# Turns of v, the keys and i by VectorE's 32 by 32 blocks and a trip through DRAM, in a hybrid RWKV-7 / HGRN2 decoder step

## The chip, the cores and the metric

The kernel runs on one core of one Trainium2 chip. The metric is the device time in microseconds (us), median of three runs: 1077.69 us before the change (1077.2 to 1079.74). A core has five engines with their own in-order instruction streams: TensorE (PE in the profile; its weight loads are PEld), VectorE (DVE), ScalarE (ACT), GpSimd (POOL) and SyncE (SP), which here only issues DMAs.

## The reference

One layer, 256 prompt tokens and 8 sequences of 8 new tokens, together NT = 320 columns; D = 2048. Cut to what matters:

```python
h = rms_norm(x, norm_g)
p = einsum('nld,dp->nlp', h, w_in)               # 2048 x 12416: most of the work
r, k, v = token-shifted columns of p             # 16 heads of 64
S_t = S_{t-1} diag(w_t) - (S_{t-1} kk_t)(kk_t a_t)^T + v_t k_t^T ;  y_t = S_t r_t     # branch A
S_t = diag(g_t) S_{t-1} + k_t i_t^T ;  o_t = S_t^T q_t                                # branch B
merged = sigmoid(gate_a) * (y_a @ proj_a) + sigmoid(gate_b) * (y_b @ proj_b)
y = x + merged @ w_out ;  final RMSNorm
```

Both recurrences are computed in chunks, as products of small matrices. All numbers are float32; a large product is three passes over a split into a high and a low part.

## The kernel before, in words

**Stages.** A start stage normalises and turns x. Then comes the recorded stage, `record_all` (lines 1533 to 1590), which fills most of the first 661 us: for each of eight pairs of heads it computes eight tiles of 128 columns of the input projection (`tile_of`, 48 matmuls into the tile `mps` each) and runs `rwkv` for two heads of branch A and `hgrn` for one of branch B. Seven further tiles, the first seven of gate a, follow the eighth pair and give TensorE something to do while the last pair ends. The last stages compute the other gates, the two branch projections (`ppa`, `ppb`) and the output projection (`po`).

**The order.** In the recorded stage nothing is issued directly. The class `Recorder` collects all operations with what they read and write (`link`), gives each an assumed cost, and lists them by a simulated greedy order (`order`); that list is then emitted, so each engine's stream is fixed when the program is built. TensorE's big matmuls keep their own order, and the products of the recurrences are set between them where their data is assumed to be ready. For a DMA that touches a DRAM scratch (names with `scr`) the recorder assumes 4.5 us until a reader may start, and 6.5 us for the large one (line 170). DMAs of this stage all stand in SP's stream, the weight loads `raw` among them.

**Turns on TensorE.** Some operands are needed with tokens in the partitions and come with tokens in the columns. `rwkv` turns v by three transposes into `pv` and two ScalarE copies into `uv` (lines 967 to 973), and the keys `bk2` and `bks` by five transposes into `pbt` and `pbs` and two copies into `bk` (1107 to 1114). `hgrn` turns i (called `v` there) by three transposes into `pvt` and two copies into `vt` (1324 to 1330). In the profile they are `bank<-ident,v`, `bank<-ident,bk`, `bank<-ident,bks` and `bank<-ident,i`.

**The inverse through DRAM.** `rwkv` inverts small triangular matrices on VectorE. The products `g2` (from `bank<-arp,bk`) are copied to `nd` (tile `big`), written to DRAM (`scr<-big`, `scrs<-dns`), read back in another layout into `U`, which is the tile `wide_` (`ww<-scr`, `ww<-scrs`), worked on by a chain of small VectorE operations, written and read again (`scr<-xc`, `ye<-scr`, `uQ<-scr`), turned in 32 by 32 blocks on VectorE (`uK<-ye`) and used in the products `bank<-yz,uE` and those behind it, the chain over chunks.

**Homes.** Tiles are buffers by tag. The tile `wide_` serves, one after the other, `uS` (columns 0 to 383), `uB` (384 to 767), `pp` with `rv` (from 768), and `U`. The tag `big` serves `nd`, `t3`, `bm` and, at the end of a pair, `sg`. Four early gates stay in `sga`; three go to DRAM (`late`, in the profile `scrg`) from buffers of `za`, `q` and `f` of the pair before the last, and come back as `ga` at line 1635. A helper emits all recorded operations, so that they have line 198 in the profile.

Of the kernel before, what the change touches and what calls it, by code (L numbers as in the profile page):

```python
# [17 lines left out]
NP_ = 256  # L18
# [22 lines left out]
NFILL = 4  # L41
NLATE = 3
# [28 lines left out]
def blocks_of(ap):  # L71

    seen = {ap.offset}
    for st, cnt in [tuple(x) for x in ap.ap]:
        if st:
            seen = {c + st * j for c in seen for j in range(cnt)}
    return ap.tensor.name, 0, 1, sum(1 << b for b in {c // 1024 for c in seen})


class Recorder:  # L80
# [17 lines left out]
    def add(self, eng, name, fn, args, kw):  # L98
# [49 lines left out]
        elif eng == "V":  # L148
# [6 lines left out]
            if name == "tensor_tensor_scan":  # L155
                o.cost = 2 * free / 0.96 + 157
        elif eng == "S":
# [269 lines left out]
def hybrid_step(ctx, tc, x_prompt, x_sample, state_rwkv, state_hgrn, state_shift, norm_g, w_in,  # L427
# [68 lines left out]
    def run(gen):  # L496
        for _ in gen:
            pass
# [323 lines left out]
    sga = ypool.tile([128, max(NFILL, 1), NT], F32, name="sga", tag="sga")  # L822
# [9 lines left out]
    def ring(pool, tag, shape, bufs, dt, size, clear=False):  # L832
# [17 lines left out]
        if len(shape) == 2:  # L850
# [4 lines left out]
    SIZES = {"uK": 384, "uS": 384, "uE": 384, "uA": 320, "uB": 384, "uQ": 320, "pp": 256, "fd": NT, "big": 512, "s0t": 512, "v": 384,  # L855
             "w1": 384, "w2": 320, "w3": 320, "ks": 128, "ket": 256, "o": NT}
# [55 lines left out]
    def rwkv(p, r, k, vp, za):  # L912
        c = lambda base: cols[:, base + p:base + p + 1]
        v = vp[:, 64:]
# [12 lines left out]
        V.tensor_scalar(kk, k, c(KK_), 0.0, op0=ALU.mult, op1=ALU.add)  # L927
# [53 lines left out]
        bk2 = at("bk2", (128, 5, 2, 64))  # L981
        blocks = bk2[:, 0:4].rearrange("p (a c) j t -> p a (c j) t", c=2)
        b64 = lambda t_: t_[:, :NP_].rearrange("p (a c t) -> p a c t", a=2, c=2)
        V.tensor_mul(blocks[:, :, 0:4:3], b64(e2), b64(be))
        V.tensor_mul(bk2[:, 4, 0], e2[:, NP_:], be[:, NP_:])
# [11 lines left out]
        V.tensor_mul(bk2[:, 4, 1], e2[:, NP_:], a[:, NP_:])  # L997
# [9 lines left out]
        bks = at("bks", (128, 2, 2, 32))  # L1007
        for a_ in range(2):
            V.tensor_mul(bks[:, a_].rearrange("p j (s i) -> p j s i", i=8),
                         bk2[:, 4, :, 32 * a_:32 * a_ + 32].rearrange("p j (s i) -> p j s i", i=8),  # L1010
                         f[:, None, 8 + 4 * a_:12 + 4 * a_, None].to_broadcast([128, 2, 4, 8]))


        az = at("az", (128, 2, 2, 96))
        rz = at("rz", (128, 4, 2, 2, 8))
        for h in range(2):
            for s_ in range(2):
# [12 lines left out]
                        bk2[HS[h], ci].rearrange("p j t -> p (j t)"), arp[HS[h], ci, :, h]),  # L1030
# [11 lines left out]
        quads = [slice(32 * q_, 32 * q_ + 32) for q_ in range(4)]  # L1042
# [120 lines left out]
        def chunks():  # L1163
            st_ = None
            for ci in range(4):
# [123 lines left out]
        sg = at("sg", tag="big")  # L1289
# [20 lines left out]
    def hgrn(hd, q, k, v, zb):  # L1310
# [186 lines left out]
    prompt_ = [scr.tile([512, 32], F32, name=f"scr{j}", tag=f"scr{j}") for j in range(2)]  # L1497
# [322 lines left out]
```

## Time and profile before

| what | value |
|---|---|
| median of three runs | 1077.69 us (1077.2 to 1079.74) |
| the profiled execution's own time | 1079.4 us |
| its span, first to last instruction | 1077.5 us |
| TensorE busy, weight loads busy | 98%, 95% of the span |
| VectorE, ScalarE, GpSimd busy | 71%, 65%, 11% |
| recorded stage | from about 27 us to about 661 us of the span |

The profile names the writing and read tiles of each instruction as out<-in. Busy matmuls overlap: a matmul's duration (about 310 ns for 320 columns) is longer than the distance to the next one, so distances of starts, not durations, add up to time.

### The profile page before, as it was taken

To read this page: it belongs to the slowest core of one execution; us is meant where nothing else is said; L and a number is where in the kernel's file an instruction comes from. 1 tells how busy PE (TensorE), PEld (TensorE's weight loads), DVE (VectorE), ACT (ScalarE), POOL (GpSimd) and SP (SyncE) were. 2 spreads that over 40 slices of the span, in tenths; PEclk is the share of its full clock that TensorE was granted. 3 is DMA by queue.
4 is the path that set the end of the run, shared out by engine and by line. 5 is a ranking of instruction groups with operands and counts; after the bars stand their busy time and mean duration, and the time that the engine had idled before them with its cause. 6 is when DMAs were issued, how large, how long until landed. Compare 5 with 4: busy or idle time off the path is not lost.

```text
span 1077.5 us, 23000 instructions
## 1 busy us (share of the span) xinstructions
PE 1057.9 (98%) x8828; PEld 1022.9 (95%) x8828; DVE 759.8 (71%) x1640; ACT 703.2 (65%) x1608; POOL 122.6 (11%) x366
## 2 busy tenths in 40 slices
PE   7999999999999999999999999999999999999996
PEld 6999999999998999999999999999999999988886
DVE  8888989988897889889898956545444444446632
ACT  7758878877967868969879778444444444434412
POOL 9410301201202112012012000000000000000000
PEclk9999999999999999999999999999999999999998
DMA  6764564563653754654735646545545555587502
GB/s 201 191 164 127 160 164 129 146 177 110 183 163 90 185 160 120 168 146 119 200 107 162 184 115 190 156 144 157 156 141 154 154 143 154 154 276 240 189 20 98
DMA packets 302353, 166.98 MB, mean 155 GB/s; under 512 B 39261, under 2 KB 291424, under 8 KB 301668
## 3 DMA queue, kind: packets, MB, share of 16 engines
q1 hardware_dynamic: 301876, 164.21, 53.7%
q8 instruction: 69, 1.13, 0.4%
q10 hardware_dynamic: 368, 1.31, 0.3%
q14 instruction: 40, 0.33, 0.1%
HBM read 154.07 MB, written 11.42 MB: 154 GB/s over the span
## 4 chain that ended last, share of the span: by engine, by line
PE 96%; DVE 1%; ACT 1%; issue 1%; DMA 1%; POOL 0%; DVEq 0%; ACTq 0%
PE mps L198 47%; PE bank L198 11%; PE mps L493 5%; PE mps L492 5%; PE mps L491 5%; PE po L1693 3%; PE po L1691 3%; PE po L1692 3%; PE ppb L492 2%; PE ppb L493 2%; PE ppb L491 2%; PE ppa L493 2%; PE ppa L492 2%; PE ppa L491 2%; PE po L1697 1%; PE po L1696 1%
## 5 line engine op out<-in xcount | busy, mean ns | idle before, releaser
L198 PE MATMUL mps<-hlo,whi 128*128 128x320 f32 x1136 | 357.5, 315 | 0.0
L198 PE MATMUL mps<-hhi,whi 128*128 128x320 f32 x1136 | 356.3, 314 | 0.0
L198 PE MATMUL mps<-hhi,wlo 128*128 128x320 f32 x1136 | 356.0, 313 | 0.0
L198 PEld LDWEIGHTS mps<-hlo,whi 128*128 128x128 f32 x1136 | 214.0, 188 | 1.7 <-issue 1.2
L198 PEld LDWEIGHTS mps<-hhi,whi 128*128 128x128 f32 x1136 | 213.9, 188 | 1.6 <-issue 0.8
L198 PEld LDWEIGHTS mps<-hhi,wlo 128*128 128x128 f32 x1136 | 214.0, 188 | 0.9 <-issue 0.4
L198 DVE TENSOR_TENSOR wlo<-raw,whi 128x1024 fp32r<-128x1024 f32 x140 | 172.0, 1228 | 20.6 <-ACT whi L198 18.3
L481 ACT CAST whi<-raw 128x1024 fp32r<-128x1024 f32 x82 | 86.1, 1051 | 146.6 <-PE mps L492 93.4
L198 ACT CAST whi<-raw 128x1024 fp32r<-128x1024 f32 x140 | 146.2, 1044 | 50.6 <-PE mps L198 45.3
L482 DVE TENSOR_TENSOR wlo<-raw,whi 128x1024 fp32r<-128x1024 f32 x82 | 100.4, 1225 | 111.1 <-ACT whi L481 111.0
L491 PE MATMUL mps<-hhi,whi 128*128 128x320 f32 x400 | 123.6, 309 | 0.0
L492 PE MATMUL mps<-hlo,whi 128*128 128x320 f32 x400 | 123.6, 309 | 0.0
L493 PE MATMUL mps<-hhi,wlo 128*128 128x320 f32 x400 | 123.6, 309 | 0.0
L491 PEld LDWEIGHTS mps<-hhi,whi 128*128 128x128 f32 x400 | 75.1, 188 | 0.0
L492 PEld LDWEIGHTS mps<-hlo,whi 128*128 128x128 f32 x400 | 75.1, 188 | 0.0
L493 PEld LDWEIGHTS mps<-hhi,wlo 128*128 128x128 f32 x400 | 75.1, 188 | 0.0
L1679 ACT CAST whi<-raw 128x1024 fp32r<-128x1024 f32 x32 | 33.2, 1051 | 47.7 <-DMA raw<-in_w_out_dram 26.0
L1680 DVE TENSOR_TENSOR wlo<-raw,whi 128x1024 fp32r<-128x1024 f32 x32 | 38.5, 1223 | 36.0 <-ACT whi L1679 30.7
L1693 PE MATMUL po<-wlo,mhi 128*128 128x512 f32 x128 | 50.1, 391 | 0.0
L1691 PE MATMUL po<-whi,mhi 128*128 128x512 f32 x128 | 50.0, 391 | 0.0
L1692 PE MATMUL po<-whi,mlo 128*128 128x512 f32 x128 | 50.0, 391 | 0.0
L492 PE MATMUL ppa<-yal,whi 128*128 128x320 f32 x128 | 39.6, 310 | 0.4 <-DVE yal L1624 0.4
(423 smaller groups left out, 2019.1 us busy)
## 6 DMA issues: line engine op xcount, KB each, us to landing
raw<-in_w_in_dram SPq DMA_DIRECT2D x194, 512.0 KB
raw<-in_w_out_dram SPq DMA_DIRECT2D x32, 512.0 KB
raw<-in_proj_a_dram SPq DMA_DIRECT2D x16, 512.0 KB
raw<-in_proj_b_dram SPq DMA_DIRECT2D x16, 512.0 KB
s<-in_state_hgrn_dram SPq DMA_DIRECT2D x8, 512.0 KB
ww<-scr SPq DMA_DIRECT2D x8, 512.0 KB
out_dram<-s SPq DMA_DIRECT2D x8, 512.0 KB
s<-in_state_rwkv_dram SPq DMA_DIRECT2D x8, 256.0 KB
```

The lines of the kernel that those rows point to most:

```text
L198: o.fn(*(real(x) for x in o.args), **{k: real(x) for k, x in o.kw.items()})
L481: S.copy(hi[:, ks], raw[:, ks])
L482: sub.tensor_sub(lo[:, ks], raw[:, ks], hi[:, ks].bitcast(F32))
L491: T.matmul(dst, hi[:, q, :], xhi[:, k, :], start=(k == 0), stop=False)
L492: T.matmul(dst, hi[:, q, :], xlo[:, k, :], start=False, stop=False)
L493: T.matmul(dst, lo[:, q, :], xhi[:, k, :], start=False, stop=(k == nk - 1))
L1679: S.copy(hi, raw)
L1680: V.tensor_sub(lo, raw, hi.bitcast(F32))
L1691: T.matmul(pt, h, hi, start=first, stop=False)
L1692: T.matmul(pt, l, hi, start=False, stop=False)
L1693: T.matmul(pt, h, lo, start=False, stop=end)
L1696: T.matmul(pt, h, hi, start=first, stop=False)
```

## The change

Per pair, the eleven transposes on TensorE and the six ScalarE copies that fetched them are gone. Instead VectorE transposes 32 by 32 blocks (`V.transpose`) of the keys (640 columns), of v (320) and of i (320); four DMAs each write the blocks to DRAM at their turned places (`turned`, `turned_i`), in pieces of 32 numbers (128 bytes); and DMAs read them back in rows of 128 numbers into `bk`, `uv` and `vt`. Keys and v go through the first 960 columns of `wide_`. `bk2` has six blocks, with the samples' keys in block 0 and `bks` in block 5. `rv` and `sg` get homes of their own (`ye`'s and a new one). All seven early gates go through DRAM, from the buffers of the last two pairs, and `sga` is gone. `kk` moves from VectorE to ScalarE, and so do the six copies per pair from PSUM into `att`. The recorder tracks DRAM scratch in blocks of 32 numbers, not 1024.

```diff
-NFILL = 4
-NLATE = 3
+NLATE = 7
...
-        V.tensor_scalar(kk, k, c(KK_), 0.0, op0=ALU.mult, op1=ALU.add)
+        S.activation(kk, k, AF.Copy, scale=c(KK_))
...
-        pv = aps("pv")
-        for w in range(3):
-            T.transpose(pv[:, 128 * w:128 * w + 128], vp[:, 128 * w:128 * w + 128], ident)
         uv = at("uv", (128, 5, 2, 64))
-        pv3 = pv[:, :384].rearrange("p (w h v) -> p w h v", w=3, h=2)
-        S.copy(uv[64:128, 0:5:2], pv3[64:128])
-        S.copy(uv[0:64, 1:5:2], pv3[0:64, 1:3])
...
+        V.transpose(wide_[:, 0:640], bk2[:, 1:6].rearrange("p s j t -> p (s j t)"))
+        V.transpose(wide_[:, 640:960], v)
+        for q_ in range(4):
+            Y.dma_start(pieces(turned)[q_], wide_[quads[q_], 0:960].rearrange("p (b c) -> p b c", c=32))
+        bk = at("bk", (128, 5, 128))
+        Y.dma_start(bk, turned[0:640].rearrange("(s p) c -> p s c", p=128))
+        tokens = turned[640:960].rearrange("(s t) c -> t s c", t=64)
+        for own, ev in ((HS[1], slice(0, 5, 2)), (HS[0], slice(1, 5, 2))):
+            Y.dma_start(uv[own, ev].rearrange("p w h v -> p w (h v)"), tokens[:, ev])
...
-        bk = at("bk", (128, 5, 128))
-        ps = aps("pbt")
-        for ci in range(4):
-            T.transpose(ps[:, 128 * ci:128 * ci + 128], bk2[:, ci].rearrange("p j t -> p (j t)"), ident)
-        S.copy(bk[:, 0:4].rearrange("p c k -> p (c k)"), ps)
-        ps = aps("pbs")
-        T.transpose(ps[:, :128], bks.rearrange("p a j t -> p (a j t)"), ident)
-        S.copy(bk[:, 4], ps[:, :128])
...
-                    rv = at("rv", (128, 3, 64), tag="pp")
+                    rv = at("rv", (128, 3, 64), tag="ye")
...
-        sg = at("sg", tag="big")
+        sg = at("sg")
...
-        ps = bps("pvt")
-        for j in range(2):
-            T.transpose(ps[:, 128 * j:128 * j + 128], v[:, 128 * j:128 * j + 128], ident)
-        T.transpose(ps[:, 256:384], v[:, NT - 128:], ident)
-        S.copy(vt[:, 0:2].rearrange("p j e -> p (j e)"), ps[:, :256])
-        S.copy(vt[0:64, 2], ps[64:128, 256:384])
+        flat = bt("flat", tag="w2")
+        V.transpose(flat, v)
+        for q_ in range(4):
+            Y.dma_start(pieces(turned_i)[q_], flat[quads[q_]].rearrange("p (b c) -> p b c", c=32))
+        Y.dma_start(vt[:, 0:2], turned_i[0:256].rearrange("(j p) c -> p j c", p=128))
+        Y.dma_start(vt[0:64, 2], turned_i[256:320])
...
-                V.tensor_copy(att[64 * b:64 * b + 32, 128 * j + 64 * b + 32:128 * j + 64 * b + 64],
+                S.copy(att[64 * b:64 * b + 32, 128 * j + 64 * b + 32:128 * j + 64 * b + 64],
                               pg[64 * j + 32 * b:64 * j + 32 * b + 32, 192:224])
-            V.tensor_copy(att[0:64, 128 * j + 64:128 * j + 128], pg[HS[j], 224:288])
+            S.copy(att[0:64, 128 * j + 64:128 * j + 128], pg[HS[j], 224:288])
...
+    pieces = lambda t_: t_.rearrange("(b x) (q c) -> q x b c", x=32, q=4)
...
-        for m in range(NFILL):
-            tile_of(OFF_GA + 128 * m, lambda ps, m=m: sigm(sga[:, m, :], ps))
-        for m, (pool, key) in enumerate(((at, "za"), (bt, "q"), (bt, "f"))[:NLATE]):
+        for m in range(NLATE):
+            pool, key = ((at, "za"), (bt, "q"), (bt, "f"))[m % 3]
```

The instruction streams change with it. First, TensorE in the first pair of heads, ahead of the products of keys with kk and r (`arp,bk`), before the change: `mps` are the big matmuls, `bank` the small PSUM buffers.

```order
L198 MATMUL mps<-hhi,wlo 128x320
L198 MATMUL mps<-hhi,whi 128x320
L198 MATMUL mps<-hlo,whi 128x320
L198 MATMUL bank_468<-ident,bk_0_510 128x128 x4
L198 MATMUL bank_464<-arp,bk_0_510 128x128
L198 MATMUL bank_465<-arp,bk_0_510 128x128
```

The same place of the changed kernel (its helper line is 199):

```order
L199 MATMUL mps<-hlo,whi 128x320
L199 MATMUL mps<-hhi,wlo 128x320
L199 MATMUL mps<-hhi,whi 128x320
L199 MATMUL bank_467<-arp,bk_0_515 128x128
L199 MATMUL bank_468<-arp,bk_0_515 128x128
```

The four transposes of the keys are gone from between the big matmuls; the same holds for the seven others of each pair.

Second, SP's stream in the first pair, before: `scr` and `scrs` are the DRAM scratch of the inverse, `w2a` small weights.

```order
L198 DMA raw<-in_w_in_dram 128x8x128 x6
L198 DMA scr_473<-big_517 32x4x32 x4
L198 DMA scrs_475<-dns_518 64x2x8
L198 DMA raw<-in_w_in_dram 128x8x128
L198 DMA w2a_0_497<-in_rwkv_w_dram 64x128
L198 DMA w2a_0_497<-in_rwkv_a_dram 64x128
L198 DMA ww<-scr_473 128x1x1024
L198 DMA ww<-scrs_475 16x8x8
```

And now, where `scrt` is the scratch for keys and v:

```order
L199 DMA raw<-in_w_in_dram 128x8x128 x3
L199 DMA scrt<-ww 32x30x32 x4
L199 DMA scr_472<-big_522 32x4x32 x4
L199 DMA scrs_476<-dns_523 64x2x8
L199 DMA raw<-in_w_in_dram 128x8x128 x2
L199 DMA uv_514<-scrt 64x3x128
L199 DMA uv_514<-scrt 64x2x128
L199 DMA bk_518<-scrt 128x5x128
L199 DMA ww<-scr_472 128x1x1024
L199 DMA ww<-scrs_476 16x8x8
```

The four writes of the turned blocks stand directly ahead of the writes of the inverse, and three reads ahead of the read of `U`. From the second pair on, weight loads stand between them.

Third, TensorE at the end of the third pair's chunks, before: `big,rhs` is the samples' state update, tiled as 64 by 64.

```order
L198 MATMUL bank_469<-rhs_539,yz 128x128
L198 MATMUL mps<-hlo,whi 128x320
L198 MATMUL mps<-hhi,wlo 128x320
L198 MATMUL bank_468<-big_517,rhs_0_540 64x256
L198 MATMUL bank_465<-big_517,rhs_0_540 64x256
```

And now:

```order
L199 MATMUL bank_468<-arp,st_549 32x64 x4
L199 MATMUL bank_468<-g_0_521,uv_514 32x64 x8
L199 MATMUL bank_468<-rz_520,s0t_516 32x16 x16
L199 MATMUL bank_463<-big_522,rhs_0_544 64x256
L199 MATMUL bank_466<-big_522,rhs_0_544 64x256
```

In the third and in the last pair that update now follows the tiled products of the outputs directly; before it stood alone between big matmuls in every pair, as it still does in the six others.

## Rows read from the trace of the kernel before

**Rows 1.** The page's first lines: the span, and each engine's busy time with its number of instructions.

```profile
span 1077.5 us, 23000 instructions
PE 1057.9 (98%) x8828; PEld 1022.9 (95%) x8828; DVE 759.8 (71%) x1640; ACT 703.2 (65%) x1608; POOL 122.6 (11%) x366
```

**Rows 2.** Stretches of the span: the recorded stage and the middle of the projections. Columns: the stretch and its length, busy us (instructions) of PE, PEld, DVE, ACT and POOL, the granted clock of TensorE, the DMA engines' busy share, GB/s.

```profile
27.00:661.40 634.40, 630.02 (x6186) 618.05 (x6186) 541.74 (x1344) 504.77 (x1303) 98.01 (x313) 1.00 0.56 151
680.00:900.00 220.00, 220.00 (x1503) 220.00 (x1502) 98.72 (x124) 97.14 (x144) 0.00 (x0) 1.00 0.52 152
```

**Rows 3.** The chain that ended last, shares by engine; and the longest entry of the waits of TensorE's weight loads in the recorded stage (total us, times, longest).

```profile
PE 96%; DVE 1%; ACT 1%; issue 1%; DMA 1%; POOL 0%; DVEq 0%; ACTq 0%
...
PEld bank L198 <- issue: 7.1, 20, 2.2
```

**Rows 4.** A piece of the chain that ended last, with nothing but big matmuls: start us, length us, what, how many. Then TensorE in order of time, around the three transposes of v in the first pair: start us, duration us, what.

```profile
37.55 8.79 PE mps L198 x60
...
61.26 0.31 PE L198 MATMUL mps<-hlo,whi 128*128 128x320 f32 x1
61.41 0.49 PE L198 MATMUL bank<-ident,v 128*128 128x128 f32 x3
61.65 0.39 PE L198 MATMUL mps<-hhi,wlo 128*128 128x320 f32 x1
61.88 0.30 PE L198 MATMUL mps<-hhi,whi 128*128 128x320 f32 x1
```

**Rows 5.** Groups of TensorE's instructions: the transposes that the change removes, with their count, busy us and mean ns of one.

```profile
L198 PE MATMUL bank<-ident,bk 128*128 128x128 f32 x32 | 4.8, 272 | 0.0
...
L198 PE MATMUL bank<-ident,v 128*128 128x128 f32 x24 | 4.2, 272 | 0.0
L198 PE MATMUL bank<-ident,i 128*128 128x128 f32 x24 | 3.9, 272 | 0.0
...
L198 PE MATMUL bank<-ident,bks 128*128 128x128 f32 x8 | 2.2, 272 | 0.0
```

**Rows 6.** TensorE in order of time, around the samples' state update of the second pair.

```profile
179.88 0.31 PE L198 MATMUL mps<-hlo,whi 128*128 128x320 f32 x1
180.12 0.66 PE L198 MATMUL bank<-big,rhs 64*64 64x256 f32 x8
180.71 0.49 PE L198 MATMUL bank<-rhs,yz 128*128 128x128 f32 x2
180.95 0.40 PE L198 MATMUL mps<-hhi,wlo 128*128 128x320 f32 x1
```

**Rows 7.** Groups of VectorE's instructions: count, busy us and mean ns of one, idle us before them.

```profile
L198 DVE COPY att<-bank 32x32 f32<-32x32 f32 (+1 forms) x48 | 9.5, 197 | 0.8
...
L198 DVE TENSOR_TENSOR q<-q,w 128x320 f32<-128x320 f32 x8 | 3.9, 490 | 2.5 <-ACT w L198 2.5
...
L198 DVE STREAM_TRANSPOSE uK<-ye 128x128 f32<-128x128 f32 x8 | 3.2, 406 | 0.0
...
L198 DVE TENSOR_SCALAR uK<-k,cols 128x320 f32<-128x320 f32 x8 | 3.1, 384 | 0.3
...
L198 DVE TENSOR_TENSOR o<-o,q 128x128 f32<-128x128 f32 x8 | 2.3, 283 | 0.0
```

**Rows 8.** Groups of ScalarE's instructions, in the same columns.

```profile
L198 ACT ACTIVATE w<-w 128x320 f32<-128x320 f32 x56 | 24.9, 467 | 0.6
...
L198 ACT ACTIVATE sf<-st,f 128x128 f32<-128x128 f32 x24 | 9.6, 402 | 1.5 <-DVE st L198 1.1
...
L198 ACT COPY bk<-bank 128x512 f32<-128x512 f32 x8 | 4.7, 582 | 2.5 <-PE bank L198 2.5
...
L198 ACT COPY bk<-bank 128x128 f32<-128x128 f32 x8 | 2.0, 256 | 0.5 <-PE bank L198 0.5
...
L198 ACT COPY o<-bank 128x64 f32<-128x64 f32 x8 | 1.6, 206 | 0.8 <-PE bank L198 0.7
```

**Rows 9.** First SP's queue: the reads of the second scratch in the third pair, in pieces of 32 numbers, as issued. Then two stretches in the columns of rows 2: one in which these pieces move, and one in which a weight load does (pieces of 128 numbers).

```profile
237.48 1.91 SPq L198 DMA_DIRECT2D uQ<-scr  x4
...
239.50:240.00 0.50, 0.50 (x6) 0.50 (x5) 0.50 (x3) 0.50 (x1) 0.00 (x0) 1.00 1.05 173
234.75:235.50 0.75, 0.75 (x7) 0.75 (x6) 0.75 (x2) 0.16 (x1) 0.00 (x0) 1.00 1.14 345
```

**Rows 10.** The read of `U` in the second pair: its issue on SP, GpSimd's first use of what landed (with its wait), VectorE's first use.

```profile
139.64 0.54 SPq L198 DMA_DIRECT2D ww<-scr  x1
...
146.90 0.17 POOL L198 MEMSET ww<- 128x40 f32 x1 [8.87 <-DMA ww<-scr]
...
147.75 0.18 DVE L198 TENSOR_TENSOR big<-ww 128x30 f32<-128x30 f32 x1
```

**Rows 11.** The end of the second pair's inverse: ScalarE's copies into `yz`, and TensorE's products with it.

```profile
170.01 0.61 ACT L198 COPY yz<-uK 32x128 f32<-32x128 f32 x2
...
171.84 0.61 PE L198 MATMUL bank<-yz,uE 128*128 128x128 f32 x4
```

**Rows 12.** The group of ScalarE's first step on a weight load in the recorded stage, with what ended the idle time before it.

```profile
L198 ACT CAST whi<-raw 128x1024 fp32r<-128x1024 f32 x140 | 146.2, 1044 | 50.6 <-PE mps L198 45.3 <-DVE wlo L198 2.3 <-issue 1.0
```

**Rows 13.** The end of the recorded stage: SP's store of the last early gate, and ScalarE's first step on branch A's output, which waits for it.

```profile
664.03 0.34 SPq L198 DMA_DIRECT2D scrg<-f  x1
...
668.10 2.62 ACT L1623 CAST yah<-ya 128x640 fp32r<-128x640 f32 x4 [1.75 <-DMA scrg<-f]
```

More of the change, by code (lines that the diff above doesn't have):

```diff
@@ L76, in blocks_of @@
             seen = {c + st * j for c in seen for j in range(cnt)}
-    return ap.tensor.name, 0, 1, sum(1 << b for b in {c // 1024 for c in seen})
+    return ap.tensor.name, 0, 1, sum(1 << b for b in {c // 32 for c in seen})
 class Recorder:
@@ L156, in add @@
                 o.cost = 2 * free / 0.96 + 157
+            if name == "transpose":
+                o.cost = free / 0.96 + 275
         elif eng == "S":
@@ L853, in ring @@
         return t_.rearrange(f"p ({' '.join(names)}) -> p {' '.join(names)}", **dict(zip(names, shape[1:])))
-    SIZES = {"uK": 384, "uS": 384, "uE": 384, "uA": 320, "uB": 384, "uQ": 320, "pp": 256, "fd": NT, "big": 512, "s0t": 512, "v": 384,
-             "w1": 384, "w2": 320, "w3": 320, "ks": 128, "ket": 256, "o": NT}
+    SIZES = {"uK": 384, "uS": 384, "uE": 384, "uA": 320, "uB": 384, "uQ": 320, "pp": 256, "fd": NT, "big": 512, "s0t": 512,
+             "w1": 384, "w2": 320, "w3": 320, "ks": 128, "ye": 192, "ket": 256, "o": NT}
     CLEAR = {"uB", "uE", "ys", "dn", "rhs", "rhs2", "k3", "vm", "w1", "vt", "att", "attc", "az", "rz"}
@@ L905, in d_tail, with rwkv @@
         return d[:, 256:328].rearrange("p (s i) -> p s i", i=9)[:, :, 1:9]
[L912 removed]
+    def rwkv(p, r, k, v, za):
         c = lambda base: cols[:, base + p:base + p + 1]
[L914 removed]
         w2a2 = at("w2a2", (128, 128))
@@ L979, in rwkv @@
         V.scalar_tensor_tensor(be, kk, -1.0, a, op0=ALU.mult, op1=ALU.mult)
-        bk2 = at("bk2", (128, 5, 2, 64))
-        blocks = bk2[:, 0:4].rearrange("p (a c) j t -> p a (c j) t", c=2)
+        bk2 = at("bk2", (128, 6, 2, 64))
+        blocks = bk2[:, 1:5].rearrange("p (a c) j t -> p a (c j) t", c=2)
         b64 = lambda t_: t_[:, :NP_].rearrange("p (a c t) -> p a c t", a=2, c=2)
         V.tensor_mul(blocks[:, :, 0:4:3], b64(e2), b64(be))
-        V.tensor_mul(bk2[:, 4, 0], e2[:, NP_:], be[:, NP_:])
+        V.tensor_mul(bk2[:, 0, 0], e2[:, NP_:], be[:, NP_:])
         c64 = lambda t_: t_.rearrange("p (c t) -> p c t", t=64)
@@ L996, in rwkv @@
         V.tensor_mul(blocks[:, :, 1:3], b64(e2), b64(a))
-        V.tensor_mul(bk2[:, 4, 1], e2[:, NP_:], a[:, NP_:])
+        V.tensor_mul(bk2[:, 0, 1], e2[:, NP_:], a[:, NP_:])
         s0t = at("s0t", (128, 4, 128))
@@ L1041, in rwkv @@
             S.copy(nd[HS[c_]], g2[HS[c_], c_:4:2, 0])
-        quads = [slice(32 * q_, 32 * q_ + 32) for q_ in range(4)]
         halves = [slice(0, 32), slice(32, 64)]
@@ L1497, in hybrid_step @@
     prompt_ = [scr.tile([512, 32], F32, name=f"scr{j}", tag=f"scr{j}") for j in range(2)]
+    turned = scr.tile([960, 128], F32, name="scrt", tag="scrt")
+    turned_i = scr.tile([NT, 128], F32, name="scri", tag="scri")
+    pieces = lambda t_: t_.rearrange("(b x) (q c) -> q x b c", x=32, q=4)
+    quads = [slice(32 * q_, 32 * q_ + 32) for q_ in range(4)]
     sample_ = [scr.tile([128, 8], F32, name=f"scrs{j}", tag=f"scrs{j}") for j in range(2)]
@@ L1563, in post @@
                 def post(ps, key=key, idx=idx):
-                    t_ = at(key, (128, 384) if key == "v" else (128, NT), bufs=BUFS[key])
+                    t_ = at(key, (128, NT), bufs=BUFS[key])
                     io[key] = t_
-                    if key == "v":
-                        G.memset(t_[:, 0:64], 0.0)
-                        t_ = t_[:, 64:]
                     shifted(idx, t_, ps)
@@ L1588, in post @@
                 Y.dma_start(late[m], t_)
-            tile_of(OFF_GA + 128 * (NFILL + m), post)
+            tile_of(OFF_GA + 128 * m, post)
         shift_state()
@@ L1629, in hybrid_step @@
     for m in range(KT):
-        if m < NFILL:
-            ga = sga[:, m, :]
-        else:
-            ga = fpr.tile([128, NT], F32, name="ga", tag="ga", bufs=2)
-            if m < NFILL + NLATE:
-                nc.sync.dma_start(ga, late[m - NFILL])
-            else:
-                run(main(OFF_GA + 128 * m, lambda ps: sigm(ga, ps)))
+        ga = fpr.tile([128, NT], F32, name="ga", tag="ga", bufs=2)
+        if m < NLATE:
+            nc.sync.dma_start(ga, late[m])
+        else:
+            run(main(OFF_GA + 128 * m, lambda ps: sigm(ga, ps)))
         gbt = fpr.tile([128, NT], F32, name="gbt", tag="gbt", bufs=2)
```

7 lines of the change are left out of this document (3 added, 4 removed).

## Prediction

> **What bounds the kernel now.** I read the page's busy shares first: TensorE is busy 98% of the span, every other engine 71% or less [rows 1]. A busy matmul is not yet a bound, so the chain of waits comes next: 96% of it is TensorE, all other engines and DMAs share the rest [rows 3]. Then the stretches, because the change lies in one stage: in the recorded stage TensorE is busy 630.0 of 634.4 us, with VectorE at 541.7 and ScalarE at 504.8 [rows 2]. So TensorE lacks 4.4 us there, and of its weight loads' waits 7.1 us in 20 places have no releaser in the profile ("issue"), 2.2 us the longest [rows 3]. The reader is to see that nobody keeps TensorE waiting there: it works through its list without pause, and what is taken out of the list shortens the stage, as long as the other engines still deliver in time. The next stage is filled in the same way, 220.0 of 220.0 us [rows 2], so a gain is not given back there.
>
> **What a removed transpose is worth.** Durations overlap, so distances of starts count. In a piece with big matmuls alone 60 take 8.79 us, 0.147 each. From the start of the three transposes at 61.41 to the start of the second big matmul behind them at 61.88 are 0.47 us; one big matmul of 0.147 lies in it, so three transposes took 0.323, 108 ns each [rows 4]. There are 32 + 24 + 24 + 8 = 88 of them [rows 5]. 88 x 0.108 = 9.5 us, all of it on the path, as no wait lies around them (idle 0.0 in each group).
>
> The groups give 272 ns as the mean duration of one [rows 5]. The Trainium skill, TensorE: Matmul & The Clock Gate, Part 4: PE-mode transpose, says that a 128 by 128 transpose takes about 275 ns in a kernel; by that figure the sum would be 24 us, and this trace has the same duration, but three of them in a row advance the stream by 323 ns, not 816. The sum goes by the distance.
>
> **Changes between tilings.** TensorE's order has one more change: the samples' state update follows other tiled products in two pairs, where it stood between full-size matmuls. In the row of such a place, from 179.88 to 180.95 are 1.07 us; one big matmul (0.147) and two full products (at the distance of a transpose, 0.108 each) lie in it, so eight passes took 0.71 us [rows 6]. Merged, they can cost between nothing and all of it less; I take 0.4 each, the middle, 0.8 us for two (0 to 1.4).
>
> **VectorE.** It loses `kk` (8 x 0.384) and the copies into `att` (48 x 0.197): 3.1 + 9.5 = 12.6 us [rows 7]. It gains turns of 640, 320 and 320 columns per pair. The trace has only 128 columns, 406 ns. If further columns cost as much as in a product (490 - 283 ns for 192 columns, 1.08 ns each), they take 0.96 + 0.61 + 0.61 = 2.18 us per pair, 17.5 in all; in proportion to columns 2.03 + 1.02 + 1.02 = 4.06, 32.5 in all. Net it is busy 4.9 to 19.9 us longer; I take the low end, as the 128 columns hold a fixed part that every VectorE row has. VectorE has 634.4 - 541.7 = 92.7 us free in the stage [rows 2], so either end is covered; without that cover it would be up to 20 us.
>
> **ScalarE.** It loses six copies per pair of 0.26 to 0.58 us [rows 8], 12 to 28 us in all. It gains 48 copies into `att` at about 0.206 (9.9 us), and `kk` with a scale per partition, which has 402 ns at 128 columns: at 320 between a plain activation's 467 ns and 1.0 us in proportion, 3.7 to 8 us in all [rows 8]. Net between 14 us less and 6 us more, and I take none; it has 634.4 - 504.8 = 130 us free [rows 2], which cover either end.
>
> **DMAs.** Per pair 13 more issues (8 writes, 5 reads) at 0.34 to 0.54 us each [rows 10, 13], 4 to 7 us of SP's time in the 79 us of a pair (634.4 / 8). Bytes: (640 + 320 + 320) x 128 x 4 = 655 KB written in 128-byte pieces and 655 KB read in 512-byte ones. In the stretch where such small pieces moved the engines carried 173 GB/s, with a weight load 345 [rows 9]: 3.8 + 1.9 = 5.7 us per pair, 7% of the stage on top of a busy share of 0.56 [rows 2]. Four more gates make 1.3 MB in all, about 4 us. Queued behind the burst of keys and v (491 KB, 2.8 us) are the weight loads and the inverse's own DMAs. The weight loads have room: ScalarE's first step on them waited 45.3 us for TensorE to free buffers, and no load is named among what ended its waits [rows 12]. So no cost from bandwidth, but see the inverse.
>
> **The added waits.** `bk`, `uv` and `vt` now arrive by DRAM: behind TensorE's products with them stand all big matmuls, as its stream is in order. The recorder sets them later, with 4.5 us per hop; the read of `U` landed 7.3 us after its issue where 6.5 were assumed, and VectorE still needed it only 0.85 us later [rows 10]; TensorE took `yz` about 1.2 us after ScalarE had written it [rows 11]. So there is about 1 us of room at each end of this chain, and a burst of 2.8 us in the same queues. In the first pair the two stand back to back, in the others weight loads lie between. Bounds: nothing, and 2.8 + 0.85 - 1 = about 3 us in every pair (24 us), both ends kept. I take 1 us in all, a third of the first pair's, because the other seven have the distance.
>
> **Other edits.** Own homes for `rv` and `sg` take waits away, from engines that are not the bound: nothing. The last gate's store still ends the stage: it was issued at 664.03, and branch A's first step waited until 668.10 for it [rows 13]; the changed kernel has the same last store behind the same number of big matmuls. The gates' reads come in a stage full of TensorE work. Nothing.
>
> **Sum.** 9.5 + 0.8 - 1.0 = 9.3 us off the profiled execution's own 1079.4 (span 1077.5, 1.9 around it): 1070.1. That execution lay 0.16% above the median of 1077.69, so the median becomes 1077.69 - 9.3 = 1068.4.
>
> **Rivals.** (a) The gain is partly eaten: each pair loses about 0.6 us more, at DRAM hops or at unexplained stalls as those of 2.2 us [rows 3]; 8 x 0.6 = 5, so 1073 (1071.5 to 1077). For it speaks the thin room of about 1 us, against it that DMAs of this chain were so far always in time. (b) The late inverse: slower. The read of `U` now waits for the burst, since both use `wide_`, and the inverse's writes queue behind it; VectorE, in order, stands before `U`, the weights' low parts stand behind it, and then TensorE starves. At 3 us in each pair 24 - 10.3 = 14 us are lost: 1091. It decides from 10.3 / 8 = 1.3 us per pair. Against it: the order of the SP stream from the second pair on. (c) TensorE's free time is filled with waiting, because something else sets the end of the stage: 1077.7. Against it stand 630.0 of 634.4 us.
>
> (d) The small pieces are far slower than I take them, so that the rings fill: at a nineteenth of 345 GB/s the burst of 491 KB takes 27 us, the inverse comes some 25 us late in each pair, and the kernel takes about 1077.7 + 200 = 1280. The Trainium skill, VectorE: DVE Perf Modes, The three transpose paths, warns that a plain DMA that transposes by strides is 19 times slower than the hardware's way. By that rule this would follow; here the 32 by 32 turns are VectorE's and the pieces stay whole, and the trace has 173 GB/s in a stretch with such pieces.
>
> **Chances.** Forecast 0.70 (1064.5 to 1071.5), (a) 0.16, (b) 0.09, (c) 0.04, (d) 0.01. A measurement of this kernel can tell 0.3%, so below 1074.5 is faster: all of the forecast and 0.10 of (a), 0.80; the same 0.06 of (a) and (c), 0.10; slower (b) and (d), 0.10. Range 1064.5, where the unexplained stalls of some 4 us also vanish, to 1076.5.
>
> **What would show it.** In the changed profile: 88 fewer transposes and TensorE still over 98.5% busy in a recorded stage of about 625 us; a turn of 640 columns on VectorE near 0.96 us (2.03 would show the other end); no entry of TensorE waiting for a DMA into `bk`, `uv` or `vt`; GpSimd's or VectorE's wait for `ww<-scr` not longer than before. Wrong would be a stage as long as before, with waits of TensorE on `yz`, `uK` or `mps`.

## The result, and the profile after

The changed kernel takes 1070.83 us (median of four runs, 1070.08 to 1071.11) against 1077.45 us before: ratio 0.9934 [0.9916, 0.9951], 6.6 us faster. A later measurement of the same two kernels gave 0.9942 [0.9928, 0.9957]. The forecast was 1068.4 us (1064.5 to 1076.5): the sign and the range were right, the gain was taken some 3 us too large.

The page of the profile after, which answers to [rows 1], with two of its DMA queues (packets, MB, share of 16 engines' span):

```profile
span 1068.6 us, 22991 instructions
PE 1047.8 (98%) x8740; PEld 1011.1 (95%) x8740; DVE 758.5 (71%) x1608; ACT 696.9 (65%) x1616; POOL 124.1 (12%) x358
...
q1 hardware_dynamic: 355892, 176.01, 60.4%
q8 instruction: 68, 1.11, 0.4%
```

The recorded stage as a stretch, in the columns of [rows 2]:

```profile
27.00:651.00 624.00, 619.33 (x6091) 605.40 (x6090) 539.23 (x1310) 498.13 (x1312) 99.64 (x305) 1.00 0.67 171
```

The chain that ended last, shares by engine, for [rows 3]:

```profile
PE 87%; ACT 4%; DVE 4%; DMA 4%; issue 1%; SPq 0%; DVEq 0%; ACTq 0%
```

TensorE has 88 matmuls fewer and is still busy 619.3 of 624.0 us. From the first to the last recorded big matmul are now 625.2 us (26.80 to 652.01), before 634.5. But the chain that ended last was 96% TensorE before and is 87% now: ScalarE, VectorE and DMAs hold it at places where they did not. The longest entries of the waits of TensorE's weight loads (total us, times, longest) show where:

```profile
PEld bank L199 <- issue: 5.0, 24, 0.6
PEld mps L199 <- issue: 3.1, 8, 0.4
PEld bank L199 <- DMA s<-in_state_rwkv_dram: 2.7, 3, 1.0
PEld bank L199 <- ACT rhs L199: 2.3, 4, 0.9
```

And ScalarE's group of the first step on a weight load, which answers to [rows 12]; below it the one wait of this kind that a load ended in the kernel before (total us, times, longest), too short for the three releasers that a group's row lists:

```profile
L199 ACT CAST whi<-raw 128x1024 fp32r<-128x1024 f32 x140 | 145.9, 1043 | 47.3 <-DMA raw<-in_w_in_dram 22.4 <-PE mps L199 19.1 <-DVE wlo L199 2.6
...
ACT whi L198 <- DMA raw<-in_w_in_dram: 0.7, 1, 0.7
```

Before, loads ended 0.7 us of the waits of ScalarE's `whi`; now they end 22.4 us of them, in 13 waits. TensorE waits 2.7 us for the state `s`. Against that, the longest wait without a releaser fell from 2.2 to 0.6 us. These three are what the experiments are about.

### The profile page after: what moved, and what is told of

Read it like the earlier page. It is cut to its first block, busy times and chain, and to the rows that moved or that the text cites. A ratio compares the mean times of both kernels' runs of the same rounds, so it can differ in the third digit from the quotient of the medians.

```text
span 1068.6 us, 22991 instructions
## 1 busy us (share of the span) xinstructions
PE 1047.8 (98%) x8740; PEld 1011.1 (95%) x8740; DVE 758.5 (71%) x1608; ACT 696.9 (65%) x1616; POOL 124.1 (12%) x358
## 4 chain that ended last, share of the span: by engine, by line
PE 87%; ACT 4%; DVE 4%; DMA 4%; issue 1%; SPq 0%; DVEq 0%; ACTq 0%
PE mps L199 39%; PE bank L199 10%; PE mps L494 5%; PE mps L493 5%; PE mps L492 5%; PE po L1678 3%; PE po L1679 3%; PE po L1680 3%; PE ppa L493 2%; PE ppb L494 2%; PE ppa L494 2%; PE ppb L493 2%; PE ppb L492 2%; PE ppa L492 2%; PE po L1684 1%; PE po L1683 1%
## 5 line engine op out<-in xcount | busy, mean ns | idle before, releaser
L199 ACT CAST whi<-raw 128x1024 fp32r<-128x1024 f32 x140 | 145.9, 1043 | 47.3 <-DMA raw<-in_w_in_dram 22.4
L492 PE MATMUL ppa<-yah,whi 128*128 128x320 f32 x128 | 39.7, 310 | 1.0 <-ACT yah L1613 1.0
```

The source lines that it names most:

```text
L199: o.fn(*(real(x) for x in o.args), **{k: real(x) for k, x in o.kw.items()})
L492: T.matmul(dst, hi[:, q, :], xhi[:, k, :], start=(k == 0), stop=False)
```

## The experiments

Times of a kernel come as a ratio to the kernel before on the same chip, with a 95% interval; 0.001 is 1.08 us. Stalls inside TensorE's stream are read as the distance between the ends of neighbouring matmuls, less the usual distance of that form.

**Both kernels again.**

> The kernel before, unchanged, to learn which of its stalls recur. Its one profile had two stalls of 1.4 and 2.2 us between small products, near 252 and 330 us of the span, with no releaser. Theory A (they belong to that one execution, which lay 2 us above the median): a second profile lacks at least one of them, its span is about 1075.5 us, and TensorE's recorded stage is about 2 us shorter than 634.4. Theory B (they belong to the program, and their absence is part of what the change gained): both stand at the same two places again and the stage takes 634 us. Ratio 1.000 in either case.

Measured: 0.9996 [0.9987, 1.0006], span 1075.0 us. TensorE in order of time shows both stalls at the same products, 1.4 and 1.5 us long (1.4 and 2.3 in the first profile):

```profile
250.71 0.30 PE L198 MATMUL bank<-o 128*32 128x32 f32 x12
252.24 0.19 PE L198 MATMUL bank<-o 128*32 128x32 f32 x1 [1.23 <-issue]
...
329.57 0.22 PE L198 MATMUL bank<-ket 128*32 128x32 f32 x2 [1.29 <-issue]
```

So the stalls belong to the program, as theory B has it, and only the length of the second varies. Span and stage, though, came as theory A has them: from the first to the last recorded big matmul are 632.0 us, 2.5 less than in the first profile. The shorter stall is 0.9 us of that. The rest lies behind it, in TensorE's granted clock: in the first profile it is 0.50, the lower of its two levels (1.2 of 2.4 GHz), for 3.4 us right behind the stall of 2.3 us, while behind the stall of 1.5 us in the second it stays at 1.00. Two stretches of the first profile, the later one for comparison, and matmuls of the earlier one:

```profile
331.00:334.00 3.00, 3.00 (x13) 3.00 (x14) 1.44 (x8) 1.62 (x7) 0.00 (x0) 0.50 0.03 5
340.00:343.00 3.00, 3.00 (x23) 3.00 (x23) 2.92 (x8) 2.91 (x10) 0.00 (x0) 1.00 0.00 0
...
333.04 0.47 PE L198 MATMUL mps<-hlo,whi 128*128 128x320 f32 x1
333.30 0.47 PE L198 MATMUL mps<-hhi,wlo 128*128 128x320 f32 x1
```

Big matmuls start 0.27 us apart there instead of 0.147, and TensorE counts as busy all the while; the mean of 1.00 in [rows 2] hides it. In the lists of the kernel before on four chips, 25 of 69 executions have a mean granted clock of 0.996 or less, and a median of 1079.7 us; the other 44 have 1077.6.

> The changed kernel, unchanged, with more rounds. Medians differed by 6.6 us, single profiles by 8.8. Theory A (9.5 us of transposes are gone, and about 3 us of new waits at DMA landings came): ratio 0.9935 to 0.9945, and a second profile shows TensorE waiting again for the state load s, 0.6 to 0.9 us, in three pairs. Theory B (the chip simply gave an unlucky set of runs, the true gain is the forecast 9.3 us): ratio 0.9914.

Measured: 0.9942 [0.9928, 0.9957], span 1068.9 us. Theory A. The new waits recur, not all at the same products: `s` once (0.9 us), the transposes of `es` twice (2.1 us) for a VectorE that was late. ScalarE's waits for weight loads are 7.5 us in all, where the first profile had 22.4 us with the same span (1068.6 us), so their total does not tell what they cost.

**The change without its turns (all_but_turns).** Its diff is that of the change, less the turns, for example:

```diff
+        S.activation(kk, k, AF.Copy, scale=c(KK_))
...
         pv = aps("pv")
         for w in range(3):
             T.transpose(pv[:, 128 * w:128 * w + 128], vp[:, 128 * w:128 * w + 128], ident)
```

> The kernel before with everything of the change except the turns: seven gates by DRAM, homes for r's value parts and the gate, kk and the att copies on ScalarE, scratch tracked in blocks of 32. v, keys and i are still turned by TensorE. Theory A (the gain is the 88 transposes at 0.108 us each): 1077.5 within 1 us of the kernel before, ratio 0.999 to 1.001. Theory B (free homes and the lighter VectorE are the gain, the turns pay for themselves only): ratio 0.994. In between, at 0.997, both halves count.

Measured: 0.9982 [0.9973, 0.9990], 1.9 us faster. Neither theory as stated. Its profile shows what was won: the stalls at 252 and 330 us are absent, and one of 0.7 us at 171 us is there in their place. That needed an explanation before anything else could be added up.

**What the stalls without a releaser are.** Counting TensorE's matmuls, weight loads and its few semaphore instructions in the trace, the two stalls of the kernel before stand at instructions 4545 and 6081, 1536 apart. Packets of 16 KB of the queue that the page calls "instruction" come one per some 256 such instructions (68 packets for 2 x 8740 matmuls and loads), and each of the stalls below whose place is given with the rest 193 ended 1.2 to 1.6 us after such a packet had landed.

```diff
-            warm(20)
+            warm(12)
+            for _ in range(52):
+                T.matmul(wps[:32, :32], ones[:, :32], ones[:, :32], start=True, stop=True)
```

> The kernel before, with its warm-up at the start changed from 20 wide to 12 wide and 52 tiny matmuls, which puts 44 more matmuls and 44 more weight loads ahead of everything else; the rest of the program keeps its order. The two stalls without releaser (1.4 and 1.5 to 2.3 us) lie 1536 = 6 x 256 TensorE instructions apart, each right behind a 16 KB packet of a queue that the profile calls 'instruction', and such packets come every 256 TensorE instructions. Theory F (TensorE waits there for its own code): with everything 88 instructions later the stalls near 250 and 329 us are gone, at most one of about 1 us stands elsewhere in a run of small tiled products, and the time falls by about 2 us, ratio 0.998. Rival P (the place in the program, its data or its banks, makes them): both stalls stand at the same products again, ratio 1.000.

Measured: 0.9992 [0.9980, 1.0004]. The two stalls are gone and two others have come, at 478 and 632 us, as TensorE in order of time has them:

```profile
476.26 0.33 PE L198 MATMUL bank<-o 128*32 128x32 f32 x14
478.36 0.27 PE L198 MATMUL bank<-ket 128*32 128x32 f32 x8 [1.77 <-issue]
...
630.30 0.38 PE L198 MATMUL bank<-rhs,yz 128*128 128x128 f32 x2
631.71 0.31 PE L198 MATMUL mps<-hlo,whi 128*128 128x320 f32 x1 [1.02 <-issue]
```

The DMA queues in the stretch from 474 to 478 us, which holds the first of them (packets, MB, share), have one code packet:

```profile
q1 hardware_dynamic: 927, 0.47, 40.3%
q8 instruction: 1, 0.02, 1.7%
```

The two new stalls stand at instructions 9153 and 12225. Divided by 256, all four leave the same rest, 193; so do the 0.7 us of the run before (3009), the 0.7 us at 545 us of the changed kernel (10433) and, in later runs, 1.9 us in early_state (8897) and 1.7 us in late_all (4801). One wait of 0.7 us without a releaser, in early_state at 616 us, has another rest (55) and stays unexplained. Rival P fell: the stall follows the block of 256 instructions, not the product. It comes where a block ends in or right behind a run of tiled products, of which TensorE had taken the last 256 instructions (128 matmuls and their loads) in 1.7 to 4.3 us; not every such end has one (none at 4545 of the run without turns, after 2.3 us, and none at 6081 of early_state, after 1.7 us). Between big matmuls it takes 128 x 0.147 = 18.8 us for as many. That the sum would shrink was wrong: there are two stalls again, 3.2 us, so the time hardly moved.

The Trainium skill, Runtime: NRT & Kernel Launch, Instruction fetch mechanics, says that an engine's code comes in 16 KiB blocks of 256 instructions and that the cost of crossing one is mostly hidden. The blocks agree with this trace; hidden they are between big matmuls, and not always behind tiled products (0.7 to 2.3 us each).

So the run without turns lacks 2.2 us of such stalls (0.7 against 2.9 in the second profile of the kernel before). That they make up its 1.9 us is argued, not shown: the streams have another order from the first pair on, and from the first to the last recorded big matmul it has 631.3 us, only 0.7 less than that profile. In the changed kernel too the stalls shrank, from 2.9 to 0.7 us, and that was not a property of the turns.

**The traffic alone.** To the run without turns only DMAs are added:

```diff
+        for q_ in range(4):
+            Y.dma_start(pieces(turned)[q_][:, 0:20], bk2[quads_[q_], 0:5].rearrange("p s j t -> p (s j t)").rearrange("p (b c) -> p b c", c=32))
+            Y.dma_start(pieces(turned)[q_][:, 20:30], v[quads_[q_]].rearrange("p (b c) -> p b c", c=32))
+        Y.dma_start(junk, turned[0:640].rearrange("(s p) c -> p s c", p=128))
...
+            Y.dma_start(pieces(turned_i)[q_], v[quads_[q_]].rearrange("p (b c) -> p b c", c=32))
+        Y.dma_start(junk[:, 3:5], turned_i[0:256].rearrange("(j p) c -> p j c", p=128))
```

> The kernel of all_but_turns (turns on TensorE) and, beside it, the DMAs that the turns through DRAM would issue: the same bytes in the same 128-byte pieces written per pair, the same reads, into a tile that nobody uses. The streams of TensorE, VectorE, ScalarE and GpSimd are word for word those of all_but_turns; only SP's stream grows by the added issues. Theory W (traffic itself delays weight loads and the inverse): 3 us or more slower than all_but_turns, ratio 1.001 or above, with ScalarE waiting for weight loads. Rival O (traffic is free; what the change lost are waits for results that now come by DRAM, and an order changed with them): as all_but_turns, 0.998.

Measured: 1.0022 [1.0012, 1.0031], which is 0.0040 (4.3 us) above the run without turns; the spans of the profiles, 1078.1 and 1073.8 us, differ by as much. Theory W, and the cleanest comparison of all, since only SP's stream differs; the traces show the instructions of TensorE, VectorE, ScalarE and GpSimd in the same order, and no fall of TensorE's clock in the stage. Waits of ScalarE and VectorE (total us, times, longest) in the run without turns:

```profile
ACT whi L199 <- DMA raw<-in_w_in_dram: 1.9, 1, 1.9
...
DVE big L199 <- DMA ww<-scr: 2.6, 1, 2.6
```

The same with the traffic, and below them those of TensorE's weight loads:

```profile
ACT whi L199 <- DMA raw<-in_w_in_dram: 10.4, 8, 2.9
...
DVE big L199 <- DMA ww<-scrs: 11.0, 7, 3.0
...
PEld bank L199 <- DVE es L199: 2.0, 2, 1.1
PEld bank L199 <- ACT i L199: 1.6, 2, 0.9
```

Weight loads land late for ScalarE, the read of `U` lands late for VectorE (in seven of eight pairs), and TensorE has new stalls at transposes of `es` and i, 1.0, 0.9, 0.9 and 0.6 us, whose operands those two engines had not finished. So TensorE gets it second hand: no row of it names a DMA here. The chain that ended last is 89% TensorE, and 95% in the run without turns. Which late load made which stall is shown for the smallest alone, at 82.9 us: the matmul's operand i was copied by ScalarE right behind a weight load's cast that had waited 0.5 us until 81.5. For the others it is argued.

**What of the traffic it is.**

```diff
-            Y.dma_start(pieces(turned)[q_], wide_[quads[q_], 0:960].rearrange("p (b c) -> p b c", c=32))
+            Y.dma_start(whole(turned)[q_], wide_[quads[q_], 0:960])
```

> The changed kernel with the same bytes of keys, v and i written to DRAM by as many DMAs, but each partition in one piece (3840 and 1280 bytes) instead of 128-byte pieces. The blocks then land at the wrong places, so this run leaves out the second half of the turn (the placing of the blocks); all instructions and waits stay. Theory W (the 128-byte pieces crowd the queues, later landings cost TensorE): ScalarE's waits for weight loads and TensorE's for the state shrink to nearly nothing, 3 to 4 us below the changed kernel, ratio about 0.991. Rival L (each landing is late by its fixed time from issue to arrival, whatever the pieces): ratio 0.994 as the changed kernel.

Measured: 0.9931 [0.9913, 0.9950], as the changed kernel; the DMA engines' busy share in the stage is 0.63 instead of 0.67, ScalarE still waits 18.8 us for weight loads and TensorE's loads 3.5 us for `s`. So longer pieces won nothing. But TensorE's products come in another order from 87 us on, so that the size of the pieces costs nothing is not shown as cleanly as the traffic's 4.3 us.

```diff
             Y.dma_start(pieces(turned)[q_], wide_[quads[q_], 0:960].rearrange("p (b c) -> p b c", c=32))
+            Y.dma_start(pieces(spare)[q_], wide_[quads[q_], 0:960].rearrange("p (b c) -> p b c", c=32))
```

> The changed kernel with the writes of keys and v to DRAM done twice, the second time to a scratch that nobody reads: 32 more writes, 3.9 MB more in 128-byte pieces, about 2.8 us of the queues per pair by the rate of 173 GB/s. Theory W (landings behind the burst are late and cost TensorE): ScalarE's waits for weight loads grow and the kernel is 3 us or more slower than the changed one, ratio 0.997 or more. Rival S (the queues have slack and the new waits have another cause): the same as the changed kernel, 0.994.

Measured: 1.0047 [1.0032, 1.0062], some 11 us above the changed kernel, ScalarE's waits for weight loads at 32.3 us. It speaks for W, but its size proves less than it seems: the second burst also holds `wide_`, so the read of `U` comes later, and the order of the products changed. Some 4 us of it are also the clock, by an estimate: behind stalls of TensorE of 2.6, 3.4 and 2.1 us (up to 83.9, 308.5 and 532.9 us) the granted clock is 0.50 to 0.51 in three stretches, in which TensorE is busy for 9.7 us; at 0.27 instead of 0.147 us per big matmul these lose 4.4 us. Whether bytes, the number of issues on SP, the in-order wait of later issues behind those for the turns or the longer hold on the tiles that they read makes the loads late stays open.

**Attempts to win the loss back.**

```diff
             o.cost, o.lat = 380, 5500
+            if any("state_rwkv" in u[0] for u in o.uses) and out.shape[1] == NSEQ and not str(aps[0].tensor.name).startswith("s_"):
+                o.lat = 9000
```

> The changed kernel with one number changed in the order's table: loads of branch A's state are assumed to take 9 us instead of 5.5, so they are issued earlier and their turns stand later. Theory W (new waits for DMA landings eat part of the gain): TensorE no longer waits for s (2.7 us in one profile, 0.9 in the other), ratio 0.992 to 0.993 instead of 0.994. Rival O (what is lost is scattered over the order of the products, and one late load only uncovers the next): the waits for s are gone, others of the same sum stand in their place, ratio 0.994.

Measured: 0.9957 [0.9945, 0.9969]. The waits for `s` are gone. Nothing is won: a wait for code of 1.9 us appeared at 473 us, and others at `es`, `rl` and `yz` (1.1, 1.2 and 1.0 us). Rival O, with chance in the placing of code on top.

```diff
-            o.cost, o.lat = 380, 5500
+            o.cost, o.lat = 380, 7500
...
-                o.lat = 6500 if out.shape[-1] == 1024 else 4500
+                o.lat = 8500 if out.shape[-1] == 1024 else 6500
```

> The changed kernel with every DMA assumed to take 2 us longer in the order's table (7.5 instead of 5.5, 6.5 and 8.5 instead of 4.5 and 6.5): loads are issued earlier, products that need them stand later. Theory W (DMA landings behind the order's assumption are what ate the gain): no wait of TensorE for s, ScalarE's waits for loads under 5 us in all, ratio 0.990 to 0.992. Rival O (more distance costs elsewhere, since the recurrences of a pair then end later and cover each other less): 0.994 or above. Whatever waits for code there are depend on where blocks of 256 TensorE instructions begin in the runs of small products, up to 2 us in either direction.

Measured: 1.0023 [1.0011, 1.0036], slower than before. No wait of TensorE names a DMA any more, ScalarE's waits for weight loads are 7.6 us (7.5 in the second profile of the changed kernel); but big matmuls now wait for ScalarE to empty their PSUM buffers (`pad`), in three places and up to 5.2 us (waits of TensorE's weight loads):

```profile
PEld mps L199 <- ACT pad L199: 9.2, 3, 5.2
```

In and behind these three stalls the granted clock is 0.50 again (404.8 to 408.0, 479.8 to 483.2 and 548.0 to 554.2 us), with 11.3 us of busy TensorE; by the same estimate some 5 us are lost there, so the stalls cost more than their length. Rival O: one price for all DMAs takes the distance from where it is needed.

```diff
+                if any(u[0].startswith(("scrt", "scri")) and not u[4] for u in o.uses):
+                    o.lat += 2000
```

> The changed kernel with one number changed: reads of the turned v, keys and i are assumed to take 6.5 us instead of 4.5, so that their users stand later in the streams. ScalarE's waits for bk and vt (6.1 us in one profile, 3.5 us the longest) hold up everything queued behind them. Theory O (late users' waits, not the traffic, ate the gain): these waits are below 1 us, ratio 0.990 to 0.992, faster than both kernels. Rival (the later place costs as much, or the waits of TensorE come from the weight loads): 0.994 or above. From where blocks of 256 TensorE instructions begin, about one wait for code near 330 us can stand.

Measured: 0.9960 [0.9948, 0.9973]. ScalarE's waits for `bk` and `vt` are gone from the profile, the time is not better: its waits for weight loads are 20.7 us, and TensorE has a wait of 2.0 us for GpSimd's `fd` at 302 us. The rival: without the waits for the turned operands the time is no better, and other waits stand there.

```diff
-NLATE = 7
+NLATE = 6
...
+                if m == NLATE:
+                    sigm(sga, ps)
+                    return
```

> The changed kernel with six early gates by DRAM and the seventh kept in a buffer on the chip. From the last recorded matmul to the first of the projection are 8.6 us in the changed kernel and 7.6 in the one before, and ScalarE's first step there waits for the last gate's store. Theory (the store, later by its landing, costs that 1.0 us): the distance is 7.6 or less and the time about 1 us below the changed kernel. Rival (the step waits for ScalarE's and VectorE's own work behind the last pair): the distance stays at 8.6.

Measured: 0.9957 [0.9943, 0.9971]. At the place itself the theory's number came: 7.2 us from the last recorded matmul to the first of the projection, and none of the waits that TensorE has there in the changed kernel, in order of time:

```profile
659.38 0.31 PE L494 MATMUL mps<-hhi,wlo 128*128 128x320 f32 x1
660.64 0.41 PE L492 MATMUL ppa<-yah,whi 128*128 128x320 f32 x1 [0.96 <-ACT yah L1613]
661.50 0.41 PE L493 MATMUL ppa<-yal,whi 128*128 128x320 f32 x1 [0.45 <-DVE yal L1614]
```

But the row of ScalarE's step in the changed kernel names another DMA, a weight load, so that the gate's store is the cause is not shown; the run without turns stores the same seven gates and has 7.7 us at this place, late_turns 7.0:

```profile
659.87 2.61 ACT L1613 CAST yah<-ya 128x640 fp32r<-128x640 f32 x4 [2.10 <-DMA raw<-in_w_in_dram]
```

The whole did not gain. The order changed in other pairs (3.9 us of waits for `s`, the longest of 2.3 us at 523 us with the granted clock at 0.50 behind it), and this profile lost 2.5 us ahead of the stage (first recorded big matmul at 29.3 instead of 26.8 us, mean granted clock 0.94 in the first 27 us), which says nothing of the gate.

**One turn back on TensorE.**

```diff
+        ps = bps("pvt")
+        for j in range(2):
+            T.transpose(ps[:, 128 * j:128 * j + 128], v[:, 128 * j:128 * j + 128], ident)
+        T.transpose(ps[:, 256:384], v[:, NT - 128:], ident)
```

> The changed kernel with only i's turn back on TensorE: 24 transposes and 16 ScalarE copies return, 8 VectorE turns, 32 writes of 128-byte pieces and 16 reads go. Theory A (0.108 us per transpose on the path): 24 x 0.108 = 2.6 us slower than the changed kernel, ratio about 0.996 to the kernel before. Theory B (the turn's DMA traffic costs TensorE as much in late loads as the transposes did): the same time as the changed kernel, ratio 0.994.

Measured: 0.9955 [0.9939, 0.9972], 1.4 us above the changed kernel of the same chip. Between the theories, and the intervals cover both. No version beat the changed kernel beyond its interval.

## Why the prediction was right, and where it was off

**The sum by runs.** Before to without turns 0.9982, then with the traffic 1.0022, then with the turns by DRAM in use 0.9942 (0.9934 in the first measurement): -1.9 us, +4.3 us, and -8.6 to -9.5 us. Each step has an interval of about 1.5 us either way. Together -6.2 to -7.1.

- **Transposes, 9.5 us:** right. The forecast had read one place. In the second profile of the kernel before 51 of the 88 stand between two big matmuls, and there they take 0.110 to 0.113 us each, for example three of i from 226.75 to 227.23 with one big matmul among them:

```profile
226.60 0.31 PE L198 MATMUL mps<-hlo,whi 128*128 128x320 f32 x1
226.75 0.49 PE L198 MATMUL bank<-ident,i 128*128 128x128 f32 x3
227.00 0.39 PE L198 MATMUL mps<-hhi,wlo 128*128 128x320 f32 x1
227.23 0.30 PE L198 MATMUL mps<-hhi,whi 128*128 128x320 f32 x1
```

  That makes 9.7 us for 88. The last of the three steps is their removal (with the merges, the copies, VectorE's turns and the new waits), and its 8.6 to 9.5 us fit. A price by the mean duration of 272 ns, 24 us, would have been far off.
- **Merged changes between tilings, 0.8 us:** mis-sized. TensorE in order of time, first around an update alone between big matmuls (second pair), then around the merged one of the third pair:

```profile
188.59 0.30 PE L199 MATMUL mps<-hhi,whi 128*128 128x320 f32 x1
188.83 0.66 PE L199 MATMUL bank<-big,rhs 64*64 64x256 f32 x8
189.42 0.41 PE L199 MATMUL mps<-hlo,whi 128*128 128x320 f32 x1
189.67 0.31 PE L199 MATMUL mps<-hhi,wlo 128*128 128x320 f32 x1
...
274.67 0.46 PE L199 MATMUL bank<-rz,s0t 128*32 128x16 f32 x32
275.06 0.66 PE L199 MATMUL bank<-big,rhs 64*64 64x256 f32 x8
275.65 0.41 PE L199 MATMUL mps<-hhi,wlo 128*128 128x320 f32 x1
275.90 0.31 PE L199 MATMUL mps<-hhi,whi 128*128 128x320 f32 x1
```

From update to next matmul are 0.59 us in both. What a merge can spare is the way in (188.59 to 188.83, 0.24, less 0.147) and one way out (189.42 to 189.67, 0.25, less 0.147): 0.1 each, 0.2 us per merge, not 0.4.

- **VectorE's turns:** covered, as said, and nearest to the low end: 0.84, 0.50 and 0.51 us, 1.84 per pair (forecast 2.18), by the groups of VectorE's instructions in the columns of [rows 7]:

```profile
L199 DVE STREAM_TRANSPOSE ww<-bk 128x640 f32<-128x640 f32 x8 | 6.7, 842 | 0.2
...
L199 DVE STREAM_TRANSPOSE w<-i 128x320 f32<-128x320 f32 x8 | 4.0, 505 | 2.0 <-ACT i L199 1.9
L199 DVE STREAM_TRANSPOSE ww<-v 128x320 f32<-128x320 f32 x8 | 4.0, 496 | 0.2
```

  VectorE as a whole was 1.3 us less busy (759.8 to 758.5), outside the forecast of 4.9 to 19.9 more; as it was not the bound, that cost the forecast nothing.

- **ScalarE:** 6.3 us less busy (703.2 to 696.9), inside the forecast of 14 less to 6 more; `kk` took 557 ns, within its bounds.
- **DMAs, "no cost from bandwidth":** this step failed. The load came out a little larger than worked out (share 0.56 to 0.67; 7% and 4 us were added in the forecast). The reason did not hold: that loads ended next to no wait of `whi` (0.7 us, which [rows 12] does not list) shows that loads were in time, not by how much. In the run with the traffic alone it cost 4.3 us, and ScalarE and VectorE waited there for weight loads and the read of `U`, 1.3 to 1.6 us each in the mean (10.4 / 8, 11.0 / 7), 3.0 the longest.
- **The added waits, 1.0 us of 0 to 24:** TensorE names no DMA into `bk`, `uv` or `vt`, as forecast. The upper bound was worked out wrongly: 2.8 + 0.85 - 1 adds the 0.85 us that are room in [rows 10]; taken off, about 1 us per pair is left, 8 us and not 24 (rival (b)'s 3 us per pair is this bound). The cost came beside these operands: at 4.3 us the two DMA terms together were 3.3 us short. With 0.4 us of the merges and 1.0 us at the stage's end, less the 1.9 us of the run without turns, that makes 2.8 us; the forecast was off by 9.3 - 6.6 = 2.7. With 1.5 us of interval in each step, that the two agree so well is luck.
- **The stage's end, "nothing":** off by 1.0 us (7.6 to 8.6 us between the stages), cause not shown.
- **The unexplained stalls:** the prediction left them in the sum and let only the range's low end have them vanish. Most of them did vanish (0.7 us of 2.9 are left), by chance of where blocks of code begin, and with them went the fall of the clock behind the longest. As far as the 1.9 us are theirs, they hid about half of the DMA term. So the total is nearer to the forecast than its parts, and that is luck.

Of the rivals, (a) had the right size of the loss per pair (4.3 / 8 = 0.54 us, forecast 0.6), but in part another place, since weight loads were late too, and not the gain of 1.9 us beside it; its 1071.5 to 1077 us were missed. (b) showed its mechanism without its price: VectorE waited for `U` up to 3.0 us with the traffic alone, and 1.1 and 2.0 us in the two profiles of the changed kernel, where it had 0.9 and 1.0 us before; so for VectorE the sign that this wait would not be longer failed. (c) and (d) did not occur.

## What to carry to other kernels

Price a removed matmul by the distance of starts, and an added DMA by a run that has the DMA alone, with all other streams unchanged: that engines hardly waited for a load says nothing of how soon they would. In a kernel with runs of many tiny matmuls, look for waits without a releaser and count instructions: a change anywhere ahead of them moves these waits, so a difference of 1 to 3 us can be an accident and has to be taken out before terms are compared. Behind a long stall, look at the granted clock in short stretches: its mean over a stage hides a fall, and the stall then costs more than its length.

## What the runs showed of the hardware that was not expected

- TensorE's waits for code: 0.7 to 2.3 us, at the same rest of 256 instructions, and only in or behind runs of tiny products; 88 instructions put ahead moved them by hundreds of us.
- TensorE's clock: behind a stall of 2.3 us the granted clock was 0.50 for 3.4 us and big matmuls stood 0.27 us apart; behind one of 1.5 us at the same products it stayed at 1.00.
- A turn of 640 columns by VectorE took 842 ns, one of 320 about 500, one of 128 columns 416: neither in proportion nor on one line.
- Bytes in 3840-byte pieces instead of 128-byte ones lowered the DMA engines' busy share from 0.67 to 0.63 and left the time where it was (with another order of the products).
